# Query and key norms moved from the attention heads into the units that project them, in one layer of a streaming encoder

## The chip, the cores and the metric

The kernel runs on one core of a Trainium2 chip. The metric is the device time of one launch in microseconds (us), as the median of several runs.

## The reference

One layer works on 576 frames (512 of a new prompt, 64 of a running stream) of width 2048:

```
hn = rmsnorm(x, g_norm1); proj = hn @ w_in          # q, k, v of 8 heads x 128, then conv columns
q = rmsnorm(q per head, g_q); k = rmsnorm(k per head, g_k)
z = q @ k_all.T / sqrt(128)                          # k_all, v_all: cache, then new rows
log_1mb = where(mask, log_sigmoid(-z), 0); after = reverse_cumsum(log_1mb) - log_1mb
w = where(mask, exp(log_sigmoid(z) + after), 0); o_attn = w @ v_all
o_conv = gb * conv3(gc * hc)
x = x + concat(rmsnorm(o_attn), rmsnorm(o_conv)) @ w_out
x = x + (silu(h2 @ w_gate) * (h2 @ w_up)) @ w_down   # h2 = rmsnorm(x, g_norm2)
```

The normed keys and the values of the new frames are outputs too. All is float32.

## The kernel before, in words

Each float32 product is made of three matmuls on TensorE (PE): the high part of the weights with the high part of the frames, the low part of the weights with the high part, and the high with the low. Frames go in two halves of 288. Splitting a weight block costs a cast on ScalarE (ACT, `hi`) and a subtraction on VectorE (DVE, `lo`).

The program up to the second projection runs in these stages.

1. The frames are read and turned, and the first projected block (`EARLY[0]`) is multiplied as they arrive. The row scale (1 over the root mean square of a frame) comes from sums that end with the frames: `row_eps` makes `eps_r` (matmul `ps_eps`, L491), `row_scale` spreads the scale over all partitions as `R1` (`ps_r`, L501).
2. Three more blocks of `EARLY` are projected plainly. `x_sums` makes sums of frame blocks beside them.
3. Units: for five heads, `UNIT_HEADS`, the query and key columns are made together by seven products in place of eight. A run is one product, eight k-steps of three matmuls. `unit_prepare` makes the weight sums and the high and low parts (`whl`, four buffers) for a run four runs ahead; `unit_run` multiplies and hands each finished half to `done`. `horder` lists the runs.
4. Ten more blocks, `LATE`, are projected plainly, and beside them the heads' attention runs. Then come conv columns, the output projection and the FFN, which are not touched.

A projected query or key goes raw to DRAM by `put_raw` into `qk_dram`. Raw means without the row scale: the RMS norm removes it, if the epsilon is scaled per frame (`eps_r`).

The order on PE and, in stages 2 to 4, on SyncE's DMA queue (SP) is the order of the code. The other engines' instructions are put in order by a scheduler. Small works stand beside the projections as generators in a `Pipeline`: a plain k-step of one half (three matmuls) is one tick, so is a unit's k-step, and `yield n` means that the rest stands n ticks later. Head `h` is spawned at tick `4 + PERIOD * h` of stage 4. Ticks of a head, counted from there, before: load q and k raw and the cached keys 0; turn q 16 and k 18 (DVE transpose, ACT square, DVE sum over 32 columns); norm q 22 and k 25 (matmul `ss` L734 for the sum over the partitions, eight small DVE operations, scaling L744, turn back L751, gain and splits `qh`, `ql`, `kh`, `kl`; POOL writes the tokens' form of k to `kb`, L746); scores `z` (L783) 39; key tokens stored 42; value tokens `vtok` loaded 56; the weights' triangular products and splits 59 to 65; `vh`, `vl`, the split of the value tokens, 66; values' product `po` (L868) 75; the end about 101. Since heads start 42 ticks apart, one head's weights fall together with the next head's turns and norms.

Values need the row scale: `values_evac` multiplies each projected half by `R1` on DVE, turns it (L1011) and stores it by four DMAs on SP.

Names in the rows: `Eq`, `Ek`, `E` are raw queries and keys; `own`, `raw_a`, `raw_g` hold weight blocks and small sums; `pr`, `ph`, `pl` are attention weights and their splits; `wlo` is a low part of a plain block.

Of the kernel before, what the change touches and what calls it, by code (L numbers as in the profile page):

```python
# [10 lines left out]
F32 = mybir.dt.float32  # L11
# [5 lines left out]
P = 128  # L17
# [81 lines left out]
def tile_hybrid_stream_step(  # L99
# [584 lines left out]
    def store_sums():  # L684
# [3 lines left out]
        for q in (1, 2, 3):  # L688
            for j in range(0, NP, 2):
                yield 12  # L690
                nc.sync.dma_start(out=xs_dram[q, j : j + 2].rearrange("j f p t -> p j f t"),
                                  in_=xf[q][:, j : j + 2].bitcast(F32))

# [19 lines left out]
    def attend(h):  # L713
        scratch = raw_tile["A"][:, 1, :]
        E = {}
        for n, j in (("q", 0), ("k", 1)):
            E[n] = t1.tile([P, T], F32, tag="E" + n, name="E" + n)
            nc.sync.dma_start(out=E[n], in_=qk_dram[2 * h + j])
        cK = t1.tile([P, TP], F32, tag="cK", name="cK")
# [3 lines left out]
        sums = {"q": scratch[:, T : T + NB], "k": scratch[:, T + 32 : T + 32 + NB]}  # L723

        def turn(n):
            nc.vector.transpose(out=E[n], in_=E[n])
            sq = scratch[:, :T]
            nc.scalar.activation(out=sq, in_=E[n], func=AF.Square)
            nc.vector.reduce_sum(out=sums[n], in_=sq.rearrange("p (b c) -> p b c", c=32), axis=mybir.AxisListType.X)

        def norm(n, gcol, e, kb=None):
            Eb = E[n].rearrange("p (b c) -> p b c", c=32)
            ss = misc("ss")[:, :NB]
            mm(ss, same, sums[n], start=True, stop=True)  # L734
            ms, t = (tmp.tile([P, HALF], F32, tag=tag, name=tag, bufs=1)[:, :NB] for tag in ("ms", "t"))
            y, r = (tmp.tile([P, HALF], F32, tag=tag, name=tag)[:, :NB] for tag in ("y", "r"))
            stt = nc.vector.scalar_tensor_tensor
            stt(out=ms, in0=ss, scalar=1.0 / P, in1=eps_r, op0=ALU.mult, op1=ALU.add)
            nc.scalar.activation(out=y, in_=ms, func=AF.Ln)
            nc.scalar.activation(out=y, in_=y, func=AF.Exp, scale=-0.5)  # L740
            stt(out=t, in0=y, scalar=-0.5, in1=y, op0=ALU.mult, op1=ALU.mult)
            nc.vector.tensor_tensor(out=t, in0=t, in1=ms, op=ALU.mult)
            stt(out=r, in0=t, scalar=1.5, in1=y, op0=ALU.add, op1=ALU.mult)
            nc.vector.tensor_tensor(out=Eb, in0=Eb, in1=r.unsqueeze(2).to_broadcast([P, NB, 32]), op=ALU.mult)  # L744
            if kb is not None:
                nc.gpsimd.tensor_tensor(out=kb.rearrange("p (b c) -> p b c", c=32), in0=Eb,  # L746
                                        in1=gk_t.unsqueeze(1).to_broadcast([P, NB, 32]), op=ALU.mult)
# [3 lines left out]
            nc.vector.transpose(out=f, in_=E[n])  # L751
# [59 lines left out]
        put_tokens(kb, kp[:, h, :], 0, TP)  # L811
        put_tokens(kb, ks[:, h, :], TP, T)
        yield 14
# [1319 lines left out]
```

## Time and profile before

| | us |
|---|---|
| median of 3 runs (2395.9 to 2398.96) | 2397.72 |
| profiled execution | 2399.18 |
| its span, first to last instruction | 2397.5 |
| PE busy | 2338.8 |
| DVE busy | 1908.4 |
| ACT busy | 1168.6 |
| POOL busy | 258.0 |

The mean granted TensorE clock was 0.99. In the trace, stage 1 ends near 39 us, stage 2 near 80, stage 3 at 191, and head 7 ends at about 480. A row of a timeline gives start, duration, engine, line, operation, tiles, shapes and, in brackets, the idle time ahead and what ended it. A row of the stretches gives, for each engine, the busy time and the number of instructions (PE, PE's weight loads, DVE, ACT, POOL), then the granted clock, the busy share of the DMA engines and GB/s. A row of the waits gives total, times and longest.

### The profile page before, as it was taken

Reading aid. Unit: us, or ns where it says so; the run is one execution under the profiler, and the core shown is the slowest. Engines: PE = TensorE matmul, PEld = TensorE weight load, DVE = VectorE, ACT = ScalarE, POOL = GpSimd, SP = SyncE. Lnnn points to the kernel's source line nnn. Section 1 sums busy time; section 2 is a strip of 40 time slices with the busy share of each in tenths; the row PEclk is TensorE's granted clock in tenths of the full one; section 3 lists DMA queues with packets and bytes.
Section 4 is the critical chain, followed back from the end, with each engine's and each line's share of the span. In section 5 each row is a group of like instructions: output and inputs, shape, how many; then the busy total and the mean of one; then the engine's idle time right before and its main releaser. Section 6 shows DMA issues by size and latency. Waiting matters only on the chain.

```text
span 2397.5 us, 43680 instructions
## 1 busy us (share of the span) xinstructions
PE 2338.8 (98%) x17453; PEld 2324.9 (97%) x17453; DVE 1908.4 (80%) x2863; ACT 1168.6 (49%) x2040; POOL 258.0 (11%) x362
## 2 busy tenths in 40 slices
PE   8998888899999999999999999999999999999999
PEld 7998878899999999999999999999999999999999
DVE  8766666688877789888888888888888877887886
ACT  7434666544445555444444444444444444444444
POOL 1001122112111131000000000000000001431121
PEclk9999899999999999999999999999999999999999
DMA  7574444395348845543444444444444855985644
GB/s 264 178 234 121 119 113 113 98 358 161 110 128 280 224 146 170 157 152 122 149 150 135 141 145 145 133 143 150 139 132 150 307 168 171 255 214 192 218 121 109
DMA packets 587476, 402.52 MB, mean 168 GB/s; under 512 B 91407, under 2 KB 575497, under 8 KB 587273
## 3 DMA queue, kind: packets, MB, share of 16 engines
q1 hardware_dynamic: 577784, 383.03, 50.9%
q0 software_dynamic: 8624, 16.22, 3.3%
q8 instruction: 136, 2.23, 0.4%
q10 hardware_dynamic: 864, 0.49, 0.1%
q14 instruction: 68, 0.55, 0.1%
HBM read 303.53 MB, written 96.16 MB: 167 GB/s over the span
## 4 chain that ended last, share of the span: by engine, by line
PE 80%; DVE 10%; ACT 3%; DMA 3%; issue 2%; POOL 1%; SPq 1%; DVEq 0%; ACTq 0%; POOLq 0%
PE psy L1783 33%; PE psw L1783 17%; PE psx L1783 8%; PE psy L1271 5%; PE pj L235 4%; PE psw L1271 3%; PE psy L950 3%; PE psw L950 1%; PE psx L1271 1%; DVE wlo L182 1%; PE po L868 1%; DMA raw_a<-in_w_out_dram 1%; PE psx L950 1%; DMA form_dram<-hf 1%; SPq L1980 1%
## 5 line engine op out<-in xcount | busy, mean ns | idle before, releaser
L1783 PE MATMUL psy<-h_s,whl 128*128 128x288 f32 x2787 | 410.8, 294 | 0.0
L1783 PEld LDWEIGHTS psy<-h_s,whl 128*128 128x128 f32 x2787 | 383.3, 188 | 0.0
L245 DVE TENSOR_TENSOR whl<-raw_a,whl 128x1024 fp32r<-128x1024 f32 (+4 forms) x296 | 318.1, 1075 | 59.1 <-ACT whl L244 58.2
L1783 PE MATMUL psw<-t,whl 128*128 128x288 f32 x2400 | 347.5, 294 | 0.0
L1783 PEld LDWEIGHTS psw<-t,whl 128*128 128x128 f32 x2400 | 327.9, 188 | 0.3 <-DVE whl L245 0.2
L244 ACT CAST whl<-raw_a 128x1024 fp32r<-128x1024 f32 (+4 forms) x296 | 267.9, 906 | 104.9 <-issue 35.4
L235 PE MATMUL pj<-x,whi 128*128 128x288 f32 x1248 | 275.2, 304 | 0.6 <-DVE x L396 0.3
L245 DVE TENSOR_TENSOR whl<-raw_b,whl 128x1024 fp32r<-128x1024 f32 (+5 forms) x190 | 196.7, 1035 | 66.5 <-ACT whl L244 65.3
L244 ACT CAST whl<-raw_b 128x1024 fp32r<-128x1024 f32 (+5 forms) x190 | 165.5, 872 | 168.4 <-issue 72.9
L1793 ACT COPY part<-psy 128x288 f32<-128x288 f32 x242 | 96.4, 398 | 284.5 <-PE psy L1783 282.4
L235 PEld LDWEIGHTS pj<-x,whi 128*128 128x128 f32 x1248 | 212.1, 194 | 2.2 <-DVE x L396 1.3
L235 PE MATMUL pj<-x,wlo 128*128 128x288 f32 x624 | 187.7, 301 | 0.1
L1783 PE MATMUL psy<-t2t,whl 128*128 128x288 f32 x1212 | 183.1, 294 | 0.0
L1783 PE MATMUL psy<-b22m,whl 128*128 128x288 f32 x1212 | 182.6, 294 | 0.0
L1783 PE MATMUL psx<-h_s,whl 128*128 128x288 f32 x1185 | 173.5, 294 | 0.0
L1783 PEld LDWEIGHTS psy<-t2t,whl 128*128 128x128 f32 x1212 | 168.2, 188 | 0.2 <-DVE whl L245 0.2
L1783 PEld LDWEIGHTS psy<-b22m,whl 128*128 128x128 f32 x1212 | 168.0, 188 | 0.0
L1783 PEld LDWEIGHTS psx<-h_s,whl 128*128 128x128 f32 x1185 | 162.6, 188 | 0.0
L235 PEld LDWEIGHTS pj<-x,wlo 128*128 128x128 f32 x624 | 120.9, 194 | 0.9 <-DVE wlo L463 0.3
L244 ACT CAST whl<-s 128x1024 fp32r<-128x1024 f32 (+5 forms) x81 | 72.3, 893 | 100.4 <-PE psw L1783 100.3
L1783 PE MATMUL psy<-t,whl 128*128 128x288 f32 x576 | 106.8, 295 | 0.3 <-ACT part L1793 0.3
L1562 POOL DMA_DIRECT2D hid_dram<-form x3 | 2.2, 748 | 971.1 <-DVE form L245 971.1
(526 smaller groups left out, 4552.5 us busy)
## 6 DMA issues: line engine op xcount, KB each, us to landing
hid_dram<-form SPq DMA_DIRECT2D x147, 288.0 KB, 2.2
raw_a<-in_w_in_dram SPq DMA_DIRECT2D x31, 1024.0 KB, 6.9
raw_a<-in_w_gate_dram SPq DMA_DIRECT2D x22, 1024.0 KB, 5.7
raw_a<-in_w_up_dram SPq DMA_DIRECT2D x22, 1024.0 KB, 6.0
raw_b<-in_w_gate_dram SPq DMA_DIRECT2D x22, 1024.0 KB, 6.5
raw_b<-in_w_up_dram SPq DMA_DIRECT2D x22, 1024.0 KB, 6.5
h_s<-hid_dram SPq DMA_DIRECT2D x10, 2016.0 KB, 9.8
raw_a<-in_w_out_dram SPq DMA_DIRECT2D x16, 1024.0 KB, 5.6
```

The source lines that it names most:

```text
L182: lo_eng.tensor_tensor(out=lo[:, a:b], in0=raw[:, a:b], in1=hi[:, a:b].bitcast(F32), op=ALU.subtract)
L235: mm(ps, w_[:, k, csl], x_, start=(k == 0 and n == 0), stop=(k == nk - 1 and n == 2))
L244: nc.scalar.copy(out=hi, in_=src)
L245: (lo_eng or nc.vector).tensor_tensor(out=lo, in0=src, in1=hi.bitcast(F32), op=ALU.subtract)
L868: mm(po[:, i * P : 512], a_[:, i, :], b_[:, : 512 - i * P], stop=(i == 0 and n == 2), **kw)
L950: mm(ps, whl[:, w_, j, :], x_, start=(start and j == 0 and q == 0), stop=(j == NP - 1 and q == 2), skip_group_check=True)
L1271: mm(ps, whl[:, w_, j, :], x_, start=(start and j == 0 and q == 0), stop=(j == m - 1 and q == 2), skip_group_check=True)
L1562: q.dma_start(out=hid_dram[fp][2 * n - 2 : 2 * n].rearrange("f p t -> p f t"), in_=t.bitcast(F32))
L1783: mm(ps, whl[:, w_, j, :], x_, start=(start and j == 0 and q == 0), stop=(j == len(xs_) - 1 and q == 2), skip_group_check=True)
L1793: nc.scalar.copy(out=t, in_=st["y"])
L1980: nc.sync.dma_start(out=y[g : g + t1 - t0, b0 : b0 + 32].rearrange("(b t) c -> t b c", t=32), in_=ap[32 * q : 32 * (q + 1), t0:t1].rearran ...
```

## The change

- `UNIT_HEADS` become heads 0 to 4 (2 to 6 before). `EARLY` holds the values of heads 0 to 3, where it held q and k of heads 0 and 1. `LATE` holds value 4 and q, k, v of heads 5 to 7. The number of blocks in each is as before.
- For a unit head, `done` turns a finished half, squares and sums it; `unit_norm`, one run after the second half, does the `ss` product, the root and the scaling, writes the normed half to `qk_dram` on POOL's queue and, for k, makes the token form and stores it. `attend` then only turns q and k back.
- Raw heads (5 to 7) keep turn and norm in `attend`, in place: one tile per q and per k in place of two. The turn back of k writes the tile that POOL reads for `kb`.
- In `attend` the value tokens are loaded earlier and split ahead of the weights; `vtok` and `cK` have two buffers; some distances change. `PERIOD` is 41.
- `row_eps` and `row_scale` come later in stage 2, since norms there are gone and values need `R1`; all `qk_dram` writes go to POOL's queue; the pipeline is not emptied at the end of the units.

```diff
@@ -38,10 +38,10 @@
 SLOTS = 7
 FORMS = 7
 STD = 2
-UNIT_HEADS = (2, 3, 4, 5, 6)
-EARLY = [(0, 0), (1, 0), (0, 1), (1, 1)]
-LATE = [(2, 0), (2, 1), (2, 2), (2, 3), (2, 4), (0, 7), (1, 7), (2, 5), (2, 6), (2, 7)]
-PERIOD = 42
+UNIT_HEADS = (0, 1, 2, 3, 4)
+EARLY = [(2, 0), (2, 1), (2, 2), (2, 3)]
+LATE = [(2, 4), (0, 5), (1, 5), (2, 5), (0, 6), (1, 6), (2, 6), (0, 7), (1, 7), (2, 7)]
+PERIOD = 41
@@ -712,59 +713,62 @@
     def attend(h):
         scratch = raw_tile["A"][:, 1, :]
-        E = {}
+        f = {}
         for n, j in (("q", 0), ("k", 1)):
-            E[n] = t1.tile([P, T], F32, tag="E" + n, name="E" + n)
-            nc.sync.dma_start(out=E[n], in_=qk_dram[2 * h + j])
-        cK = t1.tile([P, TP], F32, tag="cK", name="cK")
+            f[n] = t1.tile([P, T], F32, tag=n + "f", name=n + "f")
+            nc.sync.dma_start(out=f[n], in_=qk_dram[2 * h + j])
+        qf, kf = f["q"], f["k"]
+        cK = t1.tile([P, TP], F32, tag="cK", name="cK", bufs=2)
...
-        sums = {"q": scratch[:, T : T + NB], "k": scratch[:, T + 32 : T + 32 + NB]}
+        gcol = {"q": gqs, "k": col("gk")}
+        raw = h not in UNIT_HEADS
+        kb = t1.tile([P, T], F32, tag="kb", name="kb") if raw else None
         def turn(n):
-            nc.vector.transpose(out=E[n], in_=E[n])
+            nc.vector.transpose(out=f[n], in_=f[n])
             sq = scratch[:, :T]
-            nc.scalar.activation(out=sq, in_=E[n], func=AF.Square)
-            nc.vector.reduce_sum(out=sums[n], in_=sq.rearrange("p (b c) -> p b c", c=32), axis=mybir.AxisListType.X)
-
-        def norm(n, gcol, e, kb=None):
-            Eb = E[n].rearrange("p (b c) -> p b c", c=32)
...
-            if kb is not None:
-                nc.gpsimd.tensor_tensor(out=kb.rearrange("p (b c) -> p b c", c=32), in0=Eb,
-                                        in1=gk_t.unsqueeze(1).to_broadcast([P, NB, 32]), op=ALU.mult)
-            f = t1.tile([P, T], F32, tag=n + "f", name=n + "f")
+            y = tmp.tile([P, HALF], F32, tag="y", name="y")[:, :NB]
+            fb = f[n].rearrange("p (b c) -> p b c", c=32)
+            unit_root(scratch[:, c0 : c0 + NB], ms, y, t)
+            nc.vector.tensor_tensor(out=fb, in0=fb, in1=ms.unsqueeze(2).to_broadcast([P, NB, 32]), op=ALU.mult)
+            if n == "k":
+                key_out(kb, f[n])
+
+        def back(n, e):
             hi = t1.tile([P, e], F32R, tag=n + "h", name=n + "h")
             lo = t1.tile([P, e], F32R, tag=n + "l", name=n + "l")
-            nc.vector.transpose(out=f, in_=E[n])
-            nc.scalar.activation(out=f, in_=f, func=AF.Copy, scale=gcol)
-            split(hi, lo, f[:, :e])
-            return f, hi, lo
-
-        yield 16
-        turn("q")
-        yield 2
-        turn("k")
-        yield 4
-        qf, qh, ql = norm("q", gqs, TP)
+            nc.vector.transpose(out=f[n], in_=f[n])
+            nc.scalar.activation(out=f[n], in_=f[n], func=AF.Copy, scale=gcol[n])
+            split(hi, lo, f[n][:, :e])
+            return hi, lo
+
+        yield 14
+        if raw:
+            turn("q")
+            yield 2
+            turn("k")
+            yield 4
+            norm("q")
+        else:
+            yield 4
+        qh, ql = back("q", TP)
         yield 3
-        kb = t1.tile([P, T], F32, tag="kb", name="kb")
-        kf, kh, kl = norm("k", col("gk"), 3 * P, kb)
+        if raw:
+            norm("k")
+        kh, kl = back("k", 3 * P)
         yield 2
         nc.vector.transpose(out=cK, in_=cK)
-        yield 12
+        yield 12 if raw else 14
...
@@ -808,13 +812,16 @@
...
-        put_tokens(kb, kp[:, h, :], 0, TP)
-        put_tokens(kb, ks[:, h, :], TP, T)
-        yield 14
-        vtok = t1.tile([P, 5, P], F32, tag="vtok", name="vtok")
+        if raw:
+            put_tokens(kb, kp[:, h, :], 0, TP)
+            put_tokens(kb, ks[:, h, :], TP, T)
+        vtok = t1.tile([P, 5, P], F32, tag="vtok", name="vtok", bufs=2)
...
-        yield 2
+        yield 15
+        vh = t1.tile([P, 3, P], F32R, tag="vh", name="vh")
+        vl = t1.tile([P, 3, P], F32R, tag="vl", name="vl")
+        split(vh, vl, vtok[:, 0:3, :])
         cV = t1.tile([P, 4, P], F32, tag="cV", name="cV")
         nc.sync.dma_start(out=cV, in_=cv[:, h, :].rearrange("(i p) d -> p i d", p=P))
@@ -825,19 +832,19 @@
             nc.scalar.activation(out=pr[b], in_=z[b][:, : full[b]], func=AF.Exp)
             split(ph[b], pl[b], pb[b])
-        yield 1
+        yield 3
...
         weights(2)
-        yield 3
+        yield 4
...
         weights(1)
-        yield 3
+        yield 4
...
@@ -857,10 +864,7 @@
         split(sh, sl, sp)
...
-        vh = t1.tile([P, 3, P], F32R, tag="vh", name="vh")
-        vl = t1.tile([P, 3, P], F32R, tag="vl", name="vl")
-        split(vh, vl, vtok[:, 0:3, :])
-        yield 9
+        yield 10
...
@@ -889,6 +893,23 @@
...
+    def unit_root(sums, ms, y, t):
+
+        ss = misc("ss")[:, :NB]
+        mm(ss, same, sums, start=True, stop=True)
+        stt = nc.vector.scalar_tensor_tensor
+        stt(out=ms, in0=ss, scalar=1.0 / P, in1=eps_r, op0=ALU.mult, op1=ALU.add)
+        nc.scalar.activation(out=y, in_=ms, func=AF.Ln)
+        nc.scalar.activation(out=y, in_=y, func=AF.Exp, scale=-0.5)
+        stt(out=t, in0=y, scalar=-0.5, in1=y, op0=ALU.mult, op1=ALU.mult)
+        nc.vector.tensor_tensor(out=t, in0=t, in1=ms, op=ALU.mult)
+        stt(out=ms, in0=t, scalar=1.5, in1=y, op0=ALU.add, op1=ALU.mult)
+
+    def key_out(kb, E):
+        n = E.shape[1] // 32
+        nc.gpsimd.tensor_tensor(out=kb.rearrange("p (b c) -> p b c", c=32), in0=E.rearrange("p (b c) -> p b c", c=32),
+                                in1=gk_t.unsqueeze(1).to_broadcast([P, n, 32]), op=ALU.mult)
+
     bt = {}
     hfree, hregion, hst, hoper = [], {}, {}, {}
     NHU = len(UNIT_HEADS)
@@ -957,7 +978,21 @@
             return t
         def done(c, i, ps, part):
-            put_raw(2 * UNIT_HEADS[n] + c, ps, *HALVES[i], part)
+            t = st[c, i] = tmp.tile([P, HALF], F32, tag=("sq", "r")[c], name="E")
+            if part is not None:
+                nc.vector.tensor_tensor(out=t, in0=ps, in1=part, op=ALU.add)
+                ps = t
+            nc.vector.transpose(out=t, in_=ps)
+            sq = tmp.tile([P, HALF], F32, tag="y", name="sqE")
+            nc.scalar.activation(out=sq, in_=t, func=AF.Square)
+            if n == NHU - 1:
+                four = raw_tile["A"][:, 1, 1856 + 72 * c : 1928 + 72 * c]
+            else:
+                four = bt["small"][:, 72 * c : 72 * c + 72]
+            nc.vector.reduce_sum(out=four[:, 9 * i : 9 * i + 9], in_=sq.rearrange("p (b c) -> p b c", c=32),
+                                 axis=mybir.AxisListType.X)
+            if (c, 1 - i) in st:
+                pipe.spawn(unit_norm(UNIT_HEADS[n], c, [st[c, q] for q in range(2)], four))
         if p_ == 1:
             st["y"] = ps_pj.tile([P, HALF], F32, tag="pj", name="psy")
@@ -992,13 +1027,30 @@
...
+    def unit_norm(h, c, tiles, four):
+        yield 7
+        sums, ms, y, t = (four[:, NB * q : NB * (q + 1)] for q in range(4))
+        unit_root(sums, ms, y, t)
+        for i, (a, b) in enumerate(HALVES):
+            Eb = tiles[i].rearrange("p (b c) -> p b c", c=32)
+            nc.vector.tensor_tensor(out=Eb, in0=Eb, in1=ms[:, 9 * i : 9 * i + 9].unsqueeze(2).to_broadcast([P, 9, 32]),
+                                    op=ALU.mult)
+            nc.gpsimd.dma_start(out=qk_dram[2 * h + c][:, a:b], in_=tiles[i])
+        if c:
+            kb = rpool.tile([P, T], F32, tag="R", name="kbu", bufs=2)
+            for i, (a, b) in enumerate(HALVES):
+                key_out(kb[:, a:b], tiles[i])
+            yield 12
+            put_tokens(kb, kp[:, h, :], 0, TP)
+            put_tokens(kb, ks[:, h, :], TP, T)
+
     def put_raw(i, ps, a, b, part=None):
         t = tmp.tile([P, HALF], F32, tag="y", name="raw")
         if part is None:
             nc.scalar.copy(out=t, in_=ps)
         else:
             nc.vector.tensor_tensor(out=t, in0=ps, in1=part, op=ALU.add)
-        nc.sync.dma_start(out=qk_dram[i][:, a:b], in_=t)
+        nc.gpsimd.dma_start(out=qk_dram[i][:, a:b], in_=t)
     def raw_evac(j, h):
         return lambda ps, a, b: put_raw(2 * h + j, ps, a, b)
@@ -1022,11 +1074,24 @@
...
-    for ps, (a, b) in zip(q0ps, HALVES):
-        put_raw(0, ps, a, b)
+    def half_values(h, ps, a, b):
+        t = tmp.tile([P, HALF], F32, tag="y", name="Eh")
+        nc.vector.tensor_tensor(out=t, in0=ps, in1=R1[:, a:b], op=ALU.mult)
+        yield 3
+        nc.vector.transpose(out=t, in_=t)
+        yield 3
+        for q in range(4):
+            nc.sync.dma_start(out=vt_dram[h, a:b, 32 * q : 32 * (q + 1)].rearrange("(b t) c -> t b c", t=32),
+                              in_=t[32 * q : 32 * (q + 1), :].rearrange("t (b c) -> t b c", c=32))
+
+    def early_evac(h):
+        return lambda ps, a, b: pipe.spawn(half_values(h, ps, a, b), 14 if (h, a) == (1, 0) else 0)
+
     row_diagonals()
-    pipe.spawn(row_eps(), 4)
-    pipe.spawn(row_scale(), 10)
+    pipe.spawn(row_eps(), 23)
+    pipe.spawn(row_scale(), 26)
+    for q, (ps, (a, b)) in enumerate(zip(q0ps, HALVES)):
+        pipe.spawn(half_values(0, ps, a, b), 28 + q)
     pipe.spawn(x_sums())
...
@@ -1048,11 +1115,12 @@
     for i, (j, h) in enumerate(EARLY[1:]):
         if i == len(EARLY) - 2:
             pipe.spawn(first_units())
-        project(raw_evac(j, h), (None, "z1") if i == 0 else (None, None))
+        project(early_evac(h), (None, "z1") if i == 0 else (None, None))
     for q in (2, 3):
         unit_prepare(*horder[q])
     pipe.flush()
     pipe.spawn(store_sums())
+    stored = []
     for k_, (n, p_) in enumerate(horder):
         unit_run(n, p_)
         if k_ + 4 < len(horder):
@@ -1061,7 +1129,7 @@
             load_weight()
         if k_ == len(horder) - 3:
             split_weight(nc.vector)
-    pipe.flush()
+    assert stored
     fpool.release()
     gpool.release()
     dpool.release()
```

Two places on DVE. First, the units: here the end of one head's runs before, with the additions of finished halves (L1000) among the weight sums (L930, L931) and low parts (L927).

```order
L930 TENSOR_TENSOR raw_a<-own,raw_a 128x1024
L1000 TENSOR_TENSOR raw<-psw,part 128x288
L931 TENSOR_TENSOR own<-raw_g,own 128x1024
L927 TENSOR_TENSOR whl<-raw_a,whl 128x1024
L1000 TENSOR_TENSOR raw<-psx_1829,part 128x288
L927 TENSOR_TENSOR whl<-raw_a,whl 128x1024
```

The same place now (the sums are L951 and L952, low parts L948, additions L983; L901 to L906 are the root of q's norm):

```order
L951 TENSOR_TENSOR raw_a<-own,raw_a 128x1024
L901 SCALAR_TENSOR_TENSOR own<-ss,rpad_t 128x18
L952 TENSOR_TENSOR own<-raw_g,own 128x1024
L983 TENSOR_TENSOR E<-psw,part 128x288
L904 SCALAR_TENSOR_TENSOR own<-own 128x18
L948 TENSOR_TENSOR whl<-raw_a,whl 128x1024
L905 TENSOR_TENSOR own<-own 128x18
L985 STREAM_TRANSPOSE E<-E 128x288
L906 SCALAR_TENSOR_TENSOR own<-own 128x18
L1036 TENSOR_TENSOR E<-E,own 128x288 x2
L992 TENSOR_REDUCE own<-sqE 128x9
L948 TENSOR_TENSOR whl<-raw_a,whl 128x1024
```

Between the addition of a half and the sum that the matmul `ss` of k needs (L992) now stand a low part, the turn and two scalings of q.

Second, attention beside a unit head. Before, on DVE, the next head's norm and turn stand between the last weights and the split `vl`:

```order
L738 SCALAR_TENSOR_TENSOR ms<-ss,rpad_t 128x18
L744 TENSOR_TENSOR Eq<-Eq,r 128x576
L751 STREAM_TRANSPOSE qf<-Eq 128x576
L245 TENSOR_TENSOR pl_2799<-pr_2793,ph_2796 128x512
L741 SCALAR_TENSOR_TENSOR t<-y 128x18
L742 TENSOR_TENSOR t<-t,ms 128x18
L743 SCALAR_TENSOR_TENSOR r<-t,y 128x18
L744 TENSOR_TENSOR Ek<-Ek,r 128x576
L245 TENSOR_TENSOR ql<-qf,qh 128x512
L751 STREAM_TRANSPOSE kf<-Ek 128x576
L245 TENSOR_TENSOR kl<-kf,kh 128x384
L245 TENSOR_TENSOR vl<-vtok,vh 128x384
```

Now (L750 is the turn back, L830 and L710 belong to the weights):

```order
L245 TENSOR_TENSOR vl<-vtok,vh 128x384
L245 TENSOR_TENSOR pl_3582<-pr_3576,ph_3579 128x512
L750 STREAM_TRANSPOSE kf<-kf 128x576
L245 TENSOR_TENSOR ql<-qf,qh 128x512
L245 TENSOR_TENSOR kl<-kf,kh 128x384
L770 STREAM_TRANSPOSE cK<-cK 128x512
L830 SCALAR_TENSOR_TENSOR z_3575<-z_3575,acA 128x128 x2
L710 SCALAR_TENSOR_TENSOR raw_a<-raw_a 128x320
L245 TENSOR_TENSOR pl_3584<-pr_3578,ph_3581 128x256
```

`vl` has moved ahead of the weights, and the two scalings and eight small operations are gone from this place.

Third, DVE beside a raw head, now:

```order
L245 TENSOR_TENSOR vl<-vtok,vh 128x384
L730 STREAM_TRANSPOSE qf<-qf 128x576
L730 STREAM_TRANSPOSE kf<-kf 128x576
L734 TENSOR_REDUCE raw_a<-raw_a 128x18
L830 SCALAR_TENSOR_TENSOR z_4228<-z_4228,acA 128x128 x2
L734 TENSOR_REDUCE raw_a<-raw_a 128x18
L901 SCALAR_TENSOR_TENSOR ms<-ss,rpad_t 128x18
L710 SCALAR_TENSOR_TENSOR raw_a<-raw_a 128x320
L245 TENSOR_TENSOR pl_4237<-pr_4231,ph_4234 128x256
```

The turns and sums of the next head stay among the weights here; `vl` stands ahead of them.

More of the change, by code (lines that the diff above doesn't have):

```diff
@@ new lines, in turn, with norm @@
+            nc.scalar.activation(out=sq, in_=f[n], func=AF.Square)
+            c0 = T if n == "q" else T + 32
+            nc.vector.reduce_sum(out=scratch[:, c0 : c0 + NB], in_=sq.rearrange("p (b c) -> p b c", c=32),
+                                 axis=mybir.AxisListType.X)
+        def norm(n):
+            c0 = T if n == "q" else T + 32
+            ms, t = (tmp.tile([P, HALF], F32, tag=tag, name=tag, bufs=1)[:, :NB] for tag in ("ms", "t"))
+            y = tmp.tile([P, HALF], F32, tag="y", name="y")[:, :NB]
[4 more added lines that the diff above has]
+                key_out(kb, f[n])
@@ L1040, in first_units @@
         yield 15
-        bt["own"] = dpool.tile([P, UC], F32, tag="uc", name="own")[:, :1024].rearrange("p (j c) -> p j c", c=P)
+        own = dpool.tile([P, UC], F32, tag="uc", name="own")
+        bt["own"] = own[:, :1024].rearrange("p (j c) -> p j c", c=P)
+        bt["small"] = own[:, 1024:]
         call_blocks(range(5))
```

15 lines of the change are left out of this document (3 added, 12 removed).

## The prediction

> **What bounds the kernel now.** I read the first part of the page, then the slices, then PE's waits by stretch, then the clock right behind each wait.
>
> ```profile
> span 2397.5 us, 43680 instructions
> PE 2338.8 (98%) x17453; PEld 2324.9 (97%) x17453; DVE 1908.4 (80%) x2863; ACT 1168.6 (49%) x2040; POOL 258.0 (11%) x362
> PE   8998888899999999999999999999999999999999
> DVE  8766666688877789888888888888888877887886
> PEclk9999899999999999999999999999999999999999
> ```
>
> PE is the bound. A slice is 59.9 us, so PE dips below nine tenths only in the first slice and in slices 4 to 8, which are 180 to 480 us: the attention of the heads beside ten plain projections. From 480 us on nothing in the change touches the program, so 2397.5 moves only by what happens before. PE's waits from 185 to 480 us (total, times, longest):
>
> ```profile
> PE po L868 <- ACT vh L244: 26.8, 7, 6.1
> PE po L868 <- DVE vl L245: 7.8, 6, 1.9
> PE ss L734 <- DVE raw_a L729: 3.1, 1, 3.1
> PE z L783 <- ACT kh L244: 1.7, 2, 1.2
> PE z L783 <- DVE kl L245: 1.2, 2, 0.9
> PE os L886 <- issue: 0.8, 1, 0.8
> ```
>
> They sum to 41.4 us. 34.6 of it is one place: the values' product `po` (L868) waits in seven heads for the split `vh`, `vl` of the value tokens. That place pays twice, because the clock falls behind it. Stretches of 8 us, each from the end of one wait of 3.1 us or more (the column behind POOL's is the granted clock):
>
> ```profile
> 204.70:212.70 8.00, 7.86 (x46) 7.51 (x47) 6.99 (x19) 4.08 (x9) 1.46 (x1) 0.79 0.45 132
> 240.60:248.60 8.00, 7.26 (x33) 6.68 (x34) 2.40 (x3) 1.92 (x3) 0.00 (x0) 0.62 0.58 181
> 275.20:283.20 8.00, 7.92 (x36) 7.35 (x37) 0.60 (x2) 1.43 (x3) 0.80 (x1) 0.65 0.05 20
> 310.30:318.30 8.00, 6.16 (x21) 5.58 (x22) 3.49 (x4) 1.99 (x4) 0.80 (x1) 0.50 0.47 114
> 404.30:412.30 8.00, 6.33 (x27) 5.75 (x28) 4.41 (x7) 2.85 (x5) 0.73 (x1) 0.61 0.46 112
> 440.20:448.20 8.00, 7.20 (x36) 6.62 (x37) 2.92 (x4) 2.48 (x5) 0.81 (x1) 0.72 0.59 153
> 370.00:378.00 8.00, 5.35 (x36) 4.83 (x35) 6.30 (x13) 4.03 (x7) 2.10 (x2) 1.00 0.25 77
> ```
>
> Busy time times one minus the clock is what the slow clock costs: 1.7, 2.8, 2.8, 3.1, 2.5 and 2.0, together 14.9 us; I use 14.5, since matmul ends are modelled. The last row is head 4: it idled 2.65 us in two pieces and kept 1.00. So attention loses 41.4 + 14.5 = 56 us, and the step from a cheap wait to a dear one lies between 2.65 and 3.10 us in these rows. The Trainium skill ("TensorE: Matmul & The Clock Gate", Part 1, "What's actually happening") lets the clock fall to 4/8 only after an idle window of about 3.4 us. By that rule the 3.10 us wait would have kept its clock, and the sum would be 1.7 lower for each new wait between 3.1 and 3.4; the row of 204.70 speaks against it here, and I go by the row.
>
> Why `vh` is late: in the same ticks VectorE (DVE) does the next head's burst of turning and norming and the weight splits.
>
> ```profile
> L182 DVE TENSOR_TENSOR wlo<-raw_a,whi 128x1024 fp32r<-128x1024 f32 x26 | 31.4, 1220 | 6.3 <-ACT whi L181 6.3
> L729 DVE TENSOR_REDUCE raw_a<-raw_a 128x18 f32<-128x576 f32 x16 | 11.9, 745 | 3.5 <-ACT raw_a L728 3.3
> L744 DVE TENSOR_TENSOR Ek<-Ek,r 128x576 f32<-128x576 f32 x8 | 6.1, 756 | 0.2
> L751 DVE STREAM_TRANSPOSE kf<-Ek 128x576 f32<-128x576 f32 x8 | 6.2, 772 | 0.1
> L743 DVE SCALAR_TENSOR_TENSOR r<-t,y 128x18 f32<-128x18 f32 x16 | 2.8, 175 | 0.5
> L245 DVE TENSOR_TENSOR vl<-vtok,vh 128x384 fp32r<-128x384 f32 x8 | 5.4, 674 | 0.0
> ```
>
> **The change, part by part.** PE's work stays: the same projections, units and sixteen small sums. Terms are on the span.
>
> *Attention's old waits go:* −56. What of them returns is counted below, head by head.
>
> *Heads whose next head is a unit head (0 to 3).* The burst loses, for q and k, two turns (0.77), two reduces (0.745), two multiplications (0.756) and eight small operations (0.17): 5.9 us of DVE. The longest wait here is 5.36 us, and `vl`, last of the burst before, now stands ahead of the second weight product. Both together cover it. I charge 1 us for the four heads (0 to 6).
>
> *Start of the late projections.* The `ss` wait (3.1 and 1.7 of clock) and head 0's `z` waits go with the −56; its q and k arrive normed. Nothing new.
>
> *Heads 4, 5 and 6, whose next heads (5 to 7) stay raw.* Their burst is as before, so I carry over what these heads lost: head 4 2.65, head 5 3.92 + 1.58 and 2.3 of clock, head 6 6.06 + 0.73 and 1.8 of clock, 19 us. The wait need not stand at `po`: with `vl` early it moves on to the scores, which need the next head's `kh` and `kl`. To that comes a new wait. Before, key writing on POOL read `Ek` while DVE turned it into another tile; now the turn is in place and must wait until POOL has read.
>
> ```profile
> 237.10 1.21 POOL L746 TENSOR_TENSOR kb<-Ek,rpad_t 128x576 f32<-128x576 f32 x1 [6.12 <-DVE Ek L744]
> 348.70 0.38 PE L783 MATMUL z<-qh,kh 128*128 128x256 f32 x1 [1.16 <-ACT kh L244]
> ```
>
> It is 1.21 us here on the chain to `kl`, and the second row shows that PE waits on that chain already. Three times 1.21 is about 4, so 23 us; the ends are 15 (the early split buys back a wait per head) and 30 (each wait crosses 3.1 us). What queues behind it on DVE is the weights' and the scores' own work; nobody else.
>
> *Unit stage.* PE is fully busy here, DVE at 70 of 110 us.
>
> ```profile
> 81.00:191.00 110.00, 110.00 (x834) 110.00 (x833) 70.03 (x70) 41.55 (x54) 0.36 (x3) 1.00 0.61 195
> 127.40 1.22 DVE L930 TENSOR_TENSOR raw_a<-own,raw_g 128x1024 f32<-128x1024 f32 x1
> 128.54 0.45 DVE L1000 TENSOR_TENSOR raw<-psw,part 128x288 f32<-128x288 f32 x1
> 128.91 1.22 DVE L931 TENSOR_TENSOR own<-raw_a,own 128x1024 f32<-128x1024 f32 x1
> 130.04 1.22 DVE L927 TENSOR_TENSOR whl<-raw_a,whl 128x1024 fp32r<-128x1024 f32 x1
> ```
>
> The 35 runs of the units, from 80.1 to 191.2 us, take 3.17 us each, so a head's seven take 22. Per head come four half turns and four half reduces (0.4, half of the full ones), four half scalings (0.4) and eight small operations: about 6 us, so 20 of 22 us. It fits on average. What decides is the sum for k: PE takes `ss` one run, 3.17 us, behind the run that made its last half, and DVE has, in the new order, behind the end of that run one weight sum (start to start 1.14), the addition (0.37), a low part (1.14), the turn (0.4), two scalings (0.4 each), the reduce (0.4) and four small ones (0.5), 4.75 us, and some of the weight sum ahead: 1.6 to 2.7 us late. I take 2.3 for heads 0 to 2, whose order reads so, 1.1 for head 3 and nothing for head 4, behind which no further unit is prepared: 8 us. Ends: 0 (ACT's work is out of the chain, and runs prepared ahead hold) and 20 (q's sums late too). These waits stay below 2.65, so no clock goes. If it did, 1.7 us each would add 7.
>
> *The early part.* PE's longest wait before 185 us is this, and the clock behind it is low:
>
> ```profile
> PE ps_eps L491 <- DVE spread L486: 5.2, 1, 5.2
> 40.00:48.00 8.00, 8.00 (x42) 7.81 (x42) 7.62 (x19) 4.21 (x11) 0.00 (x0) 0.67 1.05 358
> 40.00:72.80 32.80, 32.80 (x230) 32.61 (x230) 31.27 (x72) 22.39 (x53) 0.00 (x0) 0.92 0.55 184
> 73.98 1.23 DVE L927 TENSOR_TENSOR whl<-raw_a,whl 128x1024 fp32r<-128x1024 f32 x1 [1.15 <-PE pj L235]
> ```
>
> `row_eps` moves from tick 4 to 23, so 5.2 and about 3 of clock go. But the early columns are values now: their result must be multiplied by the row scale, on DVE, which was full: eight multiplications (0.45 less overlap) and eight half turns, 5.8 us, where ACT copied before. The first two wait for the scale itself, and hold PE's bank some 1.6 us. The first unit's low part now stands behind the last of them: 72.8 + 5.8 + 1.2 is 79.8, where the units began at 80.1. PE is through at 80.1 − 8.4 + 1.6 = 73.3, waits 6 us and starts at half clock, 3 us more. Net about +2 (−4 if DVE finds gaps, +5 if a second wait follows).
>
> *Queues.* Raw q, k now leave by POOL's queue. The rows of that queue and of SP's:
>
> ```profile
> mix_dram<-mx POOLq DMA_DIRECT2D x12, 288.0 KB, 5.2
> acc<-x_dram POOLq DMA_DIRECT2D x20, 144.0 KB, 5.8
> qk_dram<-raw SPq DMA_DIRECT2D x27, 144.0 KB, 2.9
> ```
>
> A tile of a unit's half is written again about one head later; the addition that does so waits until the transfer has landed. By the order it has some 2.4 us more than 5.2, so I charge nothing; attention reads the data tens of us later. SP sheds these writes and takes eight token stores per head and four stores per early half: issues only, with nothing on PE behind them but weight loads made four runs ahead: nothing. The second buffer of `vtok` and `cK` lets loads start earlier: nothing on PE. A period of 41 instead of 42 moves head 7's end by 3 ticks, from 397 to 394: the tail runs beside conv projections either way: nothing.
>
> **Sum.** 2397.5 − 56 + 1 + 23 + 8 + 2 = 2375.5. The profiled execution took 2399.18, 1.7 more than its span and 1.5 more than the median 2397.72, so on the median's scale about 2376.
>
> **Rivals.** *Covers hold:* no unit wait, no price for the in-place turn, no loss early: 8 + 4 + 2 less, 2362. For it: DVE's 20 of 22. Against: the order of the k sum.
>
> *Units crowd:* q's sums late as well, and the clock drops: 7 for the clock or 12 for the waits' upper end (20) or something of both, 2383 to 2391. For it: two thirds of the DVE time in this stage already went without new work, and PE had no slack at all.
>
> *The wait only moves:* `pl` or `kl` is late in each of seven heads as `vh` was. Then of the 56 only the start of the late projections goes (3.1 + 1.7 and head 0's `z` waits, 1.5), and the units' 8 and the early 2 come: 2397.5 − 6.3 + 10 = 2401, within 0.2%. For it: the `z` row shows the chain to `kl` close behind. Against: 5.9 us less burst against a longest wait of 5.36.
>
> *Slower:* transfers on POOL's queue land so late that the addition of the next head's half stands on DVE, and all weight splits behind it. Its price is landing time beyond 7.6 us, once per head in five heads: from (2402.5 − 2376)/5 = 5.3 us on, that is a landing of 13 us, it ends slower; at 14.5, 2410. Against: no row above 5.8 here for this size, and DMA half idle. The Trainium skill ("DMA: Bandwidth & Descriptors", "Anatomy of one DMA — SWDGE (gpsimd) path") fits 2.0 us plus bytes over 436 GB/s, an estimate of 2.3 us for 144 KB: the rows are over twice that, so its figure is low here, but it too speaks against 13.
>
> **How the numbers follow.** Forecast 0.47, covers 0.22, crowded units 0.13, moved wait 0.09, POOL queue 0.09. The first three are faster by over 0.2% (4.8 us, about what a measurement of this kernel tells from no change): 0.82; same 0.09; slower 0.09. The forecast's own range adds its ends, raw heads 15 to 30, units 0 to 20, early −4 to +5, not all at once: 2363 to 2389. The range reaches to the covers' 2362 with their 3 us of slack, and to the crowded units: 2359 to 2392.
>
> **What would show it.** Right: no wait of `po` above 1 us in heads 0 to 3 and clock 1.00 there; `ss` waits near 2 us in three units; `ss` or `z` waits of 4 to 8 us in all for each of heads 4 to 6; a wait near 74 us. Wrong: `psw` or `psy` waiting in the units for a low part (DVE full), additions on DVE released by a transfer, or `po` still waiting for `vh` in heads 0 to 3.

## The result, and the profile after

| | before | after |
|---|---|---|
| median (4 runs each), us | 2398.2 | 2372.91 |
| profiled span, us | 2397.5 | 2372.4 |
| first unit product starts, us | 80.1 | 76.9 |
| units end (first late projection), us | 191.2 | 207.4 |
| head 7's last product, us | 480.1 | 450.5 |

The changed kernel takes 0.9895 of the time before, 95% interval 0.9877 to 0.9912: 25 us less. The page of after:

```profile
span 2372.4 us, 43758 instructions
PE 2332.3 (98%) x17453; PEld 2319.8 (98%) x17453; DVE 1916.7 (81%) x2897; ACT 1166.1 (49%) x2046; POOL 284.5 (12%) x399
PE   8899998999999999999999999999999999999999
DVE  8877667588887899888888888888888777887886
PEclk9999999999999999999999999999999999999999
```

Of slices 4 to 8, which stood below nine tenths, only slice 7 is left (356 to 415 us, raw heads); slice 2 is new (59 to 119 us, the first units). By the table the start gained 3.3 us, the units lost 19.5 (130.5 in place of 111.1), attention gained 45.8 (243.1 in place of 288.9), and the rest lost 4.5.

PE's waits of after, from 82 to 187 us and from 187 to 480 us (total, times, longest):

```profile
PE ss L899 <- DVE own L992: 8.3, 4, 2.4
PE psw L971 <- DVE part L1010: 0.3, 1, 0.3
...
PE z L787 <- ACT kh L244: 9.3, 3, 4.1
PE po L872 <- DVE pl L245: 1.2, 1, 1.2
PE ss L899 <- DVE own L992: 1.0, 1, 1.0
PE z L787 <- DVE kl L245: 0.5, 2, 0.3
PE po L872 <- ACT ph L244: 0.3, 1, 0.3
```

No `po` waits for `vh` or `vl` any more. What is left in attention are the scores `z`, three times, for `kh`: 351.12 us (4.09), 381.64 (1.95) and 413.01 (3.31), the three raw heads. New is `ss` in the units. Its waits end at 106.93 us (2.39, q of head 0) and, for k of heads 0 to 3, at 114.09 (1.97), 140.57 (1.98), 167.08 (1.99) and 191.03 (0.99). Stretches of the clock (the column behind POOL's), two long ones over the units and nine of 3.41 us around the first four waits:

```profile
84.00:120.00 36.00, 31.39 (x211) 30.69 (x210) 27.72 (x44) 13.46 (x24) 1.35 (x2) 0.91 0.57 177
120.00:207.00 87.00, 82.04 (x606) 81.34 (x605) 68.65 (x113) 35.84 (x61) 17.75 (x25) 0.98 0.62 184
104.55:107.96 3.41, 1.03 (x8) 1.03 (x9) 3.38 (x6) 0.44 (x1) 0.00 (x0) 1.00 0.00 0
107.96:111.37 3.41, 3.41 (x16) 3.41 (x16) 3.41 (x9) 1.39 (x3) 0.00 (x0) 0.50 0.57 163
111.37:114.78 3.41, 1.44 (x11) 1.21 (x10) 2.07 (x5) 1.39 (x2) 1.35 (x2) 1.00 0.92 269
114.78:118.20 3.42, 3.42 (x17) 3.42 (x15) 1.79 (x4) 0.44 (x2) 0.00 (x0) 0.50 0.99 342
138.68:142.09 3.41, 1.52 (x11) 1.52 (x12) 3.02 (x9) 1.62 (x4) 1.11 (x2) 1.00 0.87 247
142.09:145.50 3.41, 3.41 (x17) 3.41 (x16) 1.31 (x2) 0.14 (x1) 0.00 (x0) 0.50 1.11 370
162.57:165.98 3.41, 2.52 (x19) 2.29 (x18) 3.38 (x8) 2.17 (x4) 0.00 (x0) 1.00 1.10 378
165.98:169.40 3.42, 2.32 (x18) 2.33 (x19) 2.26 (x5) 0.97 (x4) 1.12 (x2) 1.00 1.14 338
169.40:172.81 3.41, 3.41 (x28) 3.41 (x27) 2.48 (x7) 0.69 (x2) 0.00 (x0) 1.00 1.10 364
```

The clock fell to half behind the first three waits, each time for 3.41 us, and not behind the fourth, which is as long as the second and third. The last section works out why.

DVE in a unit, from the end of the run that made k's last half to the sum that `ss` waits for:

```profile
135.91 1.23 DVE L952 TENSOR_TENSOR own<-raw_a,own 128x1024 f32<-128x1024 f32 x1
137.05 0.45 DVE L983 TENSOR_TENSOR E<-psw,part 128x288 f32<-128x288 f32 x1
...
137.53 1.22 DVE L948 TENSOR_TENSOR whl<-raw_a,whl 128x1024 fp32r<-128x1024 f32 x1
...
138.76 0.47 DVE L985 STREAM_TRANSPOSE E<-E 128x288 f32<-128x288 f32 x1
...
139.32 0.83 DVE L1036 TENSOR_TENSOR E<-E,own 128x288 f32<-128x288 f32 x2
140.07 0.45 DVE L992 TENSOR_REDUCE own<-sqE 128x9 f32<-128x288 f32 x1
```

It is the chain of the prediction: DVE doesn't idle in it. And the in-place turn, on POOL and on DVE, ahead of the 4.09 us wait:

```profile
347.52 1.20 POOL L910 TENSOR_TENSOR kb<-kf,rpad_t 128x576 f32<-128x576 f32 x1 [0.72 <-DVE kf L743]
348.75 0.78 DVE L750 STREAM_TRANSPOSE kf<-kf 128x576 f32<-128x576 f32 x1 [1.32 <-POOL kb L910]
```

### The profile page after: what moved, and what is told of

Same layout as the page of the kernel before. It is cut to its first block, busy times and chain, and to the rows that moved or that the text cites. A ratio compares the mean times of both kernels' runs of the same rounds, so it can differ in the third digit from the quotient of the medians.

```text
span 2372.4 us, 43758 instructions
## 1 busy us (share of the span) xinstructions
PE 2332.3 (98%) x17453; PEld 2319.8 (98%) x17453; DVE 1916.7 (81%) x2897; ACT 1166.1 (49%) x2046; POOL 284.5 (12%) x399
## 4 chain that ended last, share of the span: by engine, by line
PE 85%; DVE 7%; DMA 3%; ACT 2%; issue 1%; SPq 1%; POOL 1%; ACTq 0%; DVEq 0%; POOLq 0%
PE psy L1851 34%; PE psw L1851 17%; PE psx L1851 9%; PE psy L1339 6%; PE pj L235 5%; PE pjo L235 4%; PE psw L1339 3%; PE psy L971 2%; PE psx L1339 1%; DMA raw_a<-in_w_in_dram 1%; PE psw L971 1%; SPq L2048 1%; DVE wlo L182 1%; PE z L787 1%; DMA raw_b<-in_w_down_dram 1%
## 5 line engine op out<-in xcount | busy, mean ns | idle before, releaser
L235 PE MATMUL pj<-x,whi 128*128 128x288 f32 x1248 | 263.5, 298 | 1.4 <-DVE x L396 1.2
L235 PEld LDWEIGHTS pj<-x,whi 128*128 128x128 f32 x1248 | 204.8, 189 | 2.9 <-DVE x L396 2.4
```

Of the source, the lines that this page charges most:

```text
L235: mm(ps, w_[:, k, csl], x_, start=(k == 0 and n == 0), stop=(k == nk - 1 and n == 2))
```

## The experiments

Ratios are to the kernel before, with 95% intervals; after itself has 0.9895 (0.9877 to 0.9912). The kernel before took 2399.4 to 2400.3 us beside the runs and 2398.2 beside after, so a difference of two times is sure to some 2 us only.

**What cured `po`: the code's place of the split, the load, or the shorter burst.** First the split alone goes back behind the weights (the ticks are added here):

```diff
-        split(vh, vl, vtok[:, 0:3, :])     # tick 55, ahead of the weights
+        split(vh, vl, vtok[:, 0:3, :])     # tick 67, behind them
```

> The changed kernel, with the split vh, vl of the value tokens back behind the weights, where the kernel before has it. Theory 1 (the next head's burst was what held vh; in heads 0 to 3 the burst is 5.9 us shorter): heads 0 to 3 wait under 1.5 us each at po, heads 4 to 6 wait again at po, 2 to 4 us each with their clock: 2375 to 2385. Rival (the place of the split is what counts): all seven heads wait 4 us or more at po, and the time is near 2400.

Measured: 2371.76 us, 0.9884 (0.9871 to 0.9898), no slower. PE's waits at `po` sum to 0.6 us. The scheduler orders DVE and ACT; with the tokens there early they were split early wherever the code asked (the first `vl` starts at 239.2 us, in the changed kernel at 238.9). In heads 4 to 6, where I expected waits of 2 to 4 us, there were none for `vh` or `vl`: the forecast of this run was wrong there.

Then, in addition, the load goes back to its old tick:

```diff
+        yield 14
         vtok = ...; nc.sync.dma_start(out=vtok...)
-        yield 15
+        yield 1
```

> The kernel of the run before with the split back behind the weights, and now the load of the value tokens late too, at the tick of the kernel before. Theory 1 (the shorter burst cured po in heads 0 to 3): heads 0 to 3 still wait under 1.5 us at po, only heads 4 to 6 may wait there: 2372 to 2382. Theory 2 (the earlier load, which lets the scheduler place the split earlier, cured all seven heads): po waits for vh 3 to 6 us in seven heads and the time is 2400 or more.

```profile
PE po L873 <- DVE vl L245: 3.1, 3, 1.8
PE po L873 <- ACT vh L244: 2.4, 2, 1.2
```

Measured: 2381.39 us, 0.9928 (0.9913 to 0.9943): the early load, with the second buffer that allows it, is worth some 9 us. But most of the cure holds without it: 5.5 us of these waits in place of 34.6, in heads 0 and 6 alone. Heads 4 and 5, beside which the next head's burst is whole, wait for neither `vh` nor `vl`. So something else helps them. By the code the next head's norm of k stands 13 ticks ahead of `po` now (64 and 77) and 8 before (67 and 75), a difference of about 2 us, and the load of this run stands 23 ticks ahead of `po` where it stood 19. These distances are a likely further cause; no run sets them back.

Third, the burst alone, in the kernel before:

```diff
         def turn(n):
+            if 1 <= h <= 4:
+                return
         ...
+            if 1 <= h <= 4:
+                return norm_end(n, gcol, e, kb, Eb)    # turn back, gain, splits
             ss = misc("ss")[:, :NB]
         ...
```

> The kernel before without the turn, square, sum, root and scaling of q and k in heads 1 to 4 (that work is left out, so these heads' scores are of other numbers). Theory 1: the burst was what delayed vh, so po's waits go in heads 0 to 3 (19.6 us in the profile of before, and some 8.7 of clock) and stay in heads 4 to 6: 2370 to 2375. Theory 2 (late load of the value tokens): the split stays where it was and so do most of the waits: 2390 or more.

```profile
PE po L875 <- ACT vh L244: 16.0, 7, 6.1
PE po L875 <- DVE vl L245: 7.3, 7, 2.1
```

Measured: 2378.79 us, 0.9917 (0.9902 to 0.9932), 20 us less, though short of the 2370 to 2375 forecast. In heads 0 to 3 the two waits at `po` sum to 9.1 us where the trace of before had 19.6, and none exceeds 2.1; heads 4 to 6 wait as before (3.96, 6.09 at the longest). These heads lose 28 us there (19.6 of waits and 8.7 of clock). Of the 20 us gained 2.5 are waits at the scores and under 2 are eight small products left out; the rest is more than half of the 28. So the burst is the larger cause in heads 0 to 3. It is not the only one: in this kernel, with its late load and its distances, some 2 us per head stay.

**The start.** Two ticks in the kernel before, nothing else:

```diff
-    pipe.spawn(row_eps(), 4)
-    pipe.spawn(row_scale(), 10)
+    pipe.spawn(row_eps(), 23)
+    pipe.spawn(row_scale(), 26)
```

> The kernel before, with nothing but row_eps moved from tick 4 to 23 and row_scale from 10 to 26. Theory 1: the wait of ps_eps (5.2 us) and the clock behind it (about 3 us) go, 8 us less: 2390. Rival: the weights or sums of the next stage are what is late (DVE has 31.3 of 32.8 us full there), so the units start at 80 us as before and the time is 2398.

```profile
PE ps_r1s L501 <- DVE rpad_t L492: 2.2, 1, 2.2
```

Measured: 2394.84 us, 0.9983 (0.9974 to 0.9992), about 4 us of the 8. The wait of 5.2 us goes, and this one of 2.2 comes: the two pieces stand three ticks apart. The changed kernel has it too, and there the clock is at half behind it, from 46.5 to 49.9 us (1.7 us).

**The raw heads.** The turned k gets a tile of its own; cached keys get one buffer, to make room:

```diff
+            src = f[n]
+            if raw and n == "k":
+                f[n] = t1.tile([P, T], F32, tag="kt", name="kt")
-            nc.vector.transpose(out=f[n], in_=f[n])
+            nc.vector.transpose(out=f[n], in_=src)
```

> The changed kernel, with the turned k of heads 5 to 7 in a tile of its own, so that its turn needn't wait for POOL's reading; to make room the cached keys have one buffer. Theory 1: 1.2 to 1.3 us less wait at the scores of each of three heads and some clock, 4 to 6 us less: 2367 to 2369. Rival: the turn is late for other reasons (the norm of k starts late), PE's wait at z stays above 3 us twice, and the time stays within 2 us of 2373.

Measured: 2368.51 us, 0.9871 (0.9855 to 0.9886); in this run the scores' products of new keys in float32 read the tile before its turn. With these on the turned tile (`kf = f["k"]`):

> The changed kernel with the turned k of heads 5 to 7 in a tile of its own, which the small product of the scores reads too (the run e5 left the old tile there). As e5 measured: 2367 to 2370, 3 to 5 us under the changed kernel.

```profile
PE z L791 <- ACT kh L244: 6.0, 3, 3.0
PE z L791 <- DVE kl L245: 1.8, 3, 1.4
```

Measured: 2370.07 us, 0.988 (0.9865 to 0.9895). The scores' waits fall from 9.8 to 7.8 us, so the step on POOL is on the path; the gain of about 3 us is no larger than the intervals of the two ratios.

**The units.** First, `ss` of k later:

```diff
-        yield 7
+        yield 13 if c else 7
```

> The changed kernel, with the small product ss of k six ticks (2.4 us) later in the units; q's stays. Theory 1 (the wait is only its distance: DVE reaches the sum 2 us after PE asks, and has slack elsewhere): the four waits of k (1.97, 1.98, 1.99, 0.99) go, with their clock; head 0's q wait of 2.39 stays. 6.9 us of waits and about 3 of clock less: some 2363 us. Rival (DVE is full in the units, 20 of 22 us): the time comes back as psy or psw waiting for a low part of the weights, and 2371 to 2374 stays.

PE's waits from 82 to 210 us, and one of DVE from 82 to 207:

```profile
PE psw L971 <- DVE E L983: 5.4, 3, 2.5
PE ss L899 <- DVE own L992: 3.8, 2, 3.3
...
DVE E L983 <- DMA qk_dram<-E: 16.6, 5, 5.2
```

Measured: 2375.55 us, 0.9901 (0.9888 to 0.9915): no gain. Neither theory had it right. DVE isn't full: it stands 16.6 us on transfers, where the changed kernel has 3.7. A half's tile is written again a head later, by an addition that waits until the old contents have landed in DRAM. Scaling later means landing later, and PE then waits for the addition. It is the mechanism of my slower rival, called up by a few ticks.

Next, what these waits cost. For the half of k that is finished last (index 0), the reduce is left out in heads 1 to 3:

```diff
+            if n not in (1, 2, 3) or not c or i:
                 nc.vector.reduce_sum(out=four[:, 9 * i : 9 * i + 9], ...)
```

> The changed kernel without the sum over 32 columns of the second half of k in heads 1 to 3 (left out, so these keys are normed by an old sum), on which ss waited. Waits of 1.98, 1.99 and 0.99 go. Theory (a wait of 2 us costs only itself, as the prediction priced it): 5.0 us less, 2368. Rival (the clock falls behind these waits too, for 1.5 us or more each): 6.5 to 8 us less, 2365 to 2366.5.

```profile
PE ss L899 <- DVE own L993: 3.3, 3, 2.1
...
120.00:207.00 87.00, 85.79 (x650) 85.32 (x649) 70.14 (x121) 38.44 (x68) 17.55 (x27) 1.00 0.70 206
```

Measured: 2366.32 us, 0.9861 (0.9846 to 0.9876), 6.6 us less; the intervals of the two ratios all but touch. The waits at `ss` fell from 9.3 to 3.3 us. That is 6.0 and not the 5.0 aimed at: the wait of q of head 0 (2.39), which the edit leaves alone, is gone too, and two of 0.93 and 0.27 are new. The clock of the stretch is 1.00 where it was 0.98. The time lies in the rival's range, but its account is not what the traces show: behind the three waits that were taken away the clock had fallen once, for 1.7 us, and not each time.

Then theory 3, the chain from a half to its landed transfer. In the first version every second head's first half of k has another tile, `ss` of k comes later, `row_eps` comes behind `row_scale`, and the raw heads' k has its own tile:

```diff
-            t = st[c, i] = tmp.tile([P, HALF], F32, tag=("sq", "r")[c], name="E")
+            if c and i and n % 2:
+                t = st[c, i] = tmp.tile([P, HALF], F32, tag="acc", name="E", bufs=1)
+            else:
+                t = st[c, i] = tmp.tile([P, HALF], F32, tag=("sq", "r")[c], name="E")
...
-        yield 7
+        yield 13 if c else 7
...
-    pipe.spawn(row_eps(), 23)
+    pipe.spawn(row_eps(), 40)
```

> The changed kernel with three edits: the k tile of its own; the ss product of k six ticks later together with a tile for the first half of k in every second head that is rewritten a head later (before, the addition waited up to 5.2 us for the transfer); row_eps at tick 40, behind row_scale. Theory 3 (in the units, what counts is the chain from a finished half to its landed transfer against the next use of its tile): k's waits of 6.9 us and their clock, and the additions' waits, go; with 4 for the k tile and 2 for row_eps: 2355 to 2362. Rival (DVE is the bound in the units): PE waits for low parts instead and it stays at 2366 to 2369.

```profile
DVE E L990 <- DMA qk_dram<-E: 8.1, 3, 3.6
```

Measured: 2364.96 us, 0.986 (0.9844 to 0.9877). Better, but short of the forecast: additions still stand on transfers, `ss` still waits 6.2 us, and `row_eps` at tick 40 only exchanged its wait of 2.2 for one of 2.9 at a value's bank. The second version keeps `row_eps` at 23 and scales k into a tile of its own:

```diff
+        kn = rpool.tile([P, T], F32, tag="R", name="kn", bufs=2) if c else None
...
+            if c:
+                tiles[i] = kn[:, a:b]
```

> The run with the k tile of its own in heads 5 to 7, and in the units: the ss product of k six ticks later, the scaled k written to a tile of its own (so that a half's tile is free once it is scaled, not once its transfer has landed), the token form of k made in place. Theory 3 (chain from half to landed transfer against the next use of its tile): k's waits at ss go and no addition for k waits for a transfer; 7 us of waits and 3 to 5 of clock under 2370: 2358 to 2362. Rival (DVE or ACT is the bound in the units, whatever tile is free): waits of the same sum turn up at whl or at ss: 2367 to 2370.

```profile
DVE E L987 <- DMA qk_dram<-E: 7.8, 3, 3.0
PE ss L903 <- DVE own L996: 6.4, 5, 2.2
```

Measured: 2367.65 us, 0.9864 (0.9848 to 0.9881), in the rival's range and not in the theory's. Only q still writes from its `E`, and the additions now wait for q's transfer. So q's tiles were it as well; a third one for them:

```diff
+            if n % 2 and not c and not i:
+                t = st[c, i] = tmp.tile([P, HALF], F32, tag="acc", name="E", bufs=1)
```

> The run with k's own tile in the units, and now q's first half of every second head in a third tile, so that no addition of a finished half waits for a transfer (7.8 us, three times, in that run). Theory 3 (late sums in the units come from additions that stand on DVE behind a transfer): ss waits of heads 1 to 3 below 1 us, head 0's q stays: 3 to 6 us less, 2362 to 2365. Rival (DVE's own order delays the sums): ss waits of 2 us stay and it is 2366 to 2369.

```profile
PE ss L903 <- DVE own L999: 4.2, 2, 2.2
qk_dram<-E POOLq DMA_DIRECT2D x10, 144.0 KB, 5.6
qk_dram<-kn POOLq DMA_DIRECT2D x10, 144.0 KB, 4.5
```

Measured: 2362.08 us, 0.9837 (0.9824 to 0.9851). No addition waits for a transfer any more, though transfers land later than in the changed kernel (5.6 against 3.6), and `ss` waits twice: 1.96 (head 0's q) and 2.23. That second one I had expected below 1; what delays it I didn't settle. This version beats both kernels; against after the intervals don't touch.

**The queue.** The scaled halves by SP in place of POOL:

```diff
-            nc.gpsimd.dma_start(out=qk_dram[2 * h + c][:, a:b], in_=tiles[i])
+            nc.sync.dma_start(out=qk_dram[2 * h + c][:, a:b], in_=tiles[i])
```

> The changed kernel with the units' scaled halves written by SP's queue in place of POOL's. The prediction's term (queues cost nothing): 2371 to 2375, as the changed kernel. Rival 1 (POOL's queue lands late and delays the next use of the tile): 2 to 6 us less. Rival 2 (SP stands on the scaled half, and the weight loads behind it come late): 5 us more or above, with low parts waiting for weights.

```profile
SPq L1038 <- DVE E L1036: 29.7, 8, 10.5
...
PE zs L811 <- DVE cK L770: 1.7, 1, 1.7
PE pj L235 <- ACT whi L181: 1.1, 1, 1.1
```

Measured: 2383.43 us, 0.9925 (0.9911 to 0.9938), slower than after by 10 us in the medians and 7 by the ratios, whose intervals just touch. On SP the same transfer lands in 2.8 us, but the queue stands 29.7 us for the scaling, and the loads behind it come late: in attention weights and cached keys are then waited for.

## Why the prediction was right, point by point

*The sum.* 2376 was forecast and 2372.91 measured, but the terms are off in both directions and cancel. On the span, attention came out 13.8 us better than its terms (45.8 gained against 56 − 1 − 23), the units 11.5 worse, the early part 5.3 better, and 4.5 were lost behind attention, where nothing was forecast. That the total came within 3 us is luck.

*Attention's waits go.* Right, and it is nearly all of the gain. The 41.4 us of waits became 11.3 (the rows above without `ss`, which is still a unit's). The price of the clock was right: busy time times one minus the clock, summed over pieces of half a us, is 14.3 before, where I used 14.5, and 5.6 after. With ten small products that moved to the units (under 2.4) and five ticks (2.0, see below) that is about 43 of the 45.8; the rest I can't place.

*Heads 0 to 3.* Right in the sum and half right in the cause. The 5.9 us of burst is the main one (e7: 20 us); the split's place ahead of the weights, to which I gave the other part, does nothing in itself (e4). What does is the earlier load with a second buffer (e6: 9 us), which I had costed at nothing, and probably the longer distances, which I had not costed either.

*Heads 4 to 6.* The mechanism was as told: waits moved from `po` to the scores, and the turn stands behind POOL, 1.32 us by the trace against 1.21 forecast. The size was high: 11.3 us of waits, and 5.6 of clock behind them, 17 in place of 23.

*Units: the term that was mis-sized.* 8 us were forecast; the stage takes 19.5 more. The waits themselves were near: k's 1.97, 1.98, 1.99 and 0.99, forecast 2.3 three times and 1.1, and none in head 4. Missed were head 0's q (2.39), the clock, and ten small products that moved here from attention (0.24 us each at most, so under 2.4, which attention gained). The step that failed worst is "these waits stay below 2.65, so no clock goes": the clock fell three times ((1 − 0.91) × 31.4 + (1 − 0.98) × 82.0 is 4.5 us). With 1.2 at the first unit and 0.3 at `psw` that makes about 18 of the 19.5.

*The early part.* The step that failed is that DVE, full, would hold the first unit for 6 us and leave a cold clock. It waited 0.8 us ahead of its first product and 1.2 behind it, at a clock of 1.00; the start came out 3.3 us earlier rather than 2 later. The new wait of 2.2 at `ps_r1s`, with 1.7 of clock, was not seen.

*Queues.* Nothing, as said, and the runs show how near that was: additions stood 3.7 us on transfers in the changed kernel without reaching PE, and 16.6 in e2, where they did. The rival priced landing as a sum of 13 us; a scaling that comes 2.4 us later did it at ordinary landings (3.8 us at the median). How long a landing takes belongs to the stretch: by the same queue and at the same size the units' halves of the changed kernel took 3.6, the raw halves of heads 5 to 7 took 2.3.

*What was not in the sum.* From head 7's end on the changed kernel lost 4.5 us: 2.0 are the five ticks by which its head 7 ends earlier in the program (its last product stands at tick 390 of stage 4 where it stood at 395; the prediction counted three), 1.6 are longer waits behind 480 us, mostly for low parts of weights (2.5 in place of 1.3). The remaining 0.9 I can't place.

## What to carry to other kernels

Work that is moved off a crowded stage has to be priced where it lands by its latency chain, not by the busy share of the engine: DVE had idle time in the units, and still the k sums of heads 0 to 2 came 2 us late. A tile that is stored from in place is in use until the store has landed, so scaling into a tile of its own, or a third buffer, may be worth more than moving the waiting instruction. Where a scheduler orders an engine, look at what data arrives when, not at the place of the instruction in the code.

## What the runs showed of the hardware that I had not expected

The falls of the clock stand on a fixed raster. In the rows shown with the result the stretches at 0.50 begin at 107.96, 114.78 and 142.09 us and last 3.41 us; the distances, 6.82 and 27.31, are 2 and 8 times 3.41. Cut into pieces of 3.41 us on this raster, the trace shows what decides: PE's idle time within the piece ahead. It is 2.38, 1.97 and 1.89 us ahead of the three falls. The wait of 1.99 us that ends at 167.08 lies across an edge, with 0.89 in one piece and 1.10 in the next, and the clock stayed at 1.00. Head 4's 2.65 us in the kernel before, from which I had taken my bound, lie across an edge too, with 1.16 and 1.49:

```profile
369.55:372.96 3.41, 2.25 (x16) 1.86 (x14) 3.34 (x9) 2.20 (x6) 0.56 (x1) 1.00 0.28 90
372.96:376.37 3.41, 1.92 (x11) 1.78 (x12) 2.12 (x2) 1.22 (x3) 1.02 (x1) 1.00 0.10 16
```

Between 24 and 480 us the other traces agree: behind pieces at full clock with at most 1.5 us idle none falls, from 1.9 us on all do, and between the two some do (1.68 in e4, piece from 162.73) and some don't (1.79 in e6, from 350.23). The edges are read from the falls themselves, to about 0.05 us. So no step lies between 2.65 and 3.10. From about 2 us on a wait can cost 1.7 us more, and where it falls on the raster decides. The program does not set that: in the changed kernel the third k wait of the units (1.99 us) left the clock alone, in e4, with the same units, it was 2.02 us long and brought a fall. A difference of 2 us between two versions can come from this alone. The Trainium skill ("TensorE: Matmul & The Clock Gate", Part 1, "What's actually happening") gives an idle window of about 3.4 us as the condition; the traces here show falls behind shorter idle times, while that the window runs freely agrees with falls that differ for equal waits.
